# A hybrid attention and delta-rule layer on one core: the first weights fetched behind two input tiles, and the first two weight jobs' column blocks in another order

## Chip, core and metric

The kernel runs on one core of one Trainium2 chip. The metric is device time in microseconds of the whole launch; several runs are taken and their median is given. A profiled execution of the same kernel gives the rows quoted here; its times count from the start of its span.

## What is computed

The reference is one layer of a streaming encoder. A prompt of 2048 rows and a sample of 32 rows, each row 1024 wide, are normalised, projected by one wide matrix, sent through two branches (chunk-band attention and a gated delta rule) and merged:

```python
hp = layer_norm(x_prompt, ln0_g, ln0_b)          # 2048 x 1024
hs = layer_norm(x_sample, ln0_g, ln0_b)          #   32 x 1024
# in trunk_layer, for either of them:
qa, ka, va, za, qkv_b, zb, a_b, b_b, gate_a, gate_b = split_projection(x @ w_in)
...
mix = jax.nn.sigmoid(gate_a) * ya + jax.nn.sigmoid(gate_b) * yb
y = layer_norm(ALPHA * x + mix @ w_out, ln_g, ln_b)
```

Only the first step matters for this change: the normalisation of the first rows and the first products `x @ w_in`, which belong to the logits `gate_a` and `gate_b`.

## The kernel before

The projection is made weight tile by weight tile, the weights stationary in TensorE and the transposed rows moving: a **job** is one block of 128 columns of `w_in` (1024 x 128, 512 KB), multiplied with half of the rows. The prompt is split in two halves of 1024 rows; what follows is the first half. The rows come as eight input tiles x0 to x7 of 128 rows (512 KB each).

**Building h** (`build_h`, lines 465 to 560). For each input tile: a transfer into `x`; on VectorE two `bn_stats`, one `bn_aggr`, one small addition; on GpSimd the power -0.5; on VectorE the subtraction and scaling of the whole tile ("x<-x,mv" in the trace); on TensorE eight transposes, four into a bank of the tag `b` and four into one of the tag `a`; then ScalarE applies gain and bias to the first four (`tmp<-b`) and VectorE to the other four (`tmp<-a`); ScalarE casts `tmp` to f16 (`hi`), GpSimd forms the rest (`lo<-tmp,hi`). A column block of a job can start when `hi` of its tiles is there and ends with eight products that read `lo`.

**Fetching and dividing weights** (`fetch`, line 583; `divide`, line 613). `fetch` issues two transfers of 256 KB for each job into one of two `wraw` buffers. `divide` handles one job after the other: ScalarE squares the tile and sums it, a small product with `tiny` sums over partitions (`b<-w_sq,tiny`), then `w_scale` goes through VectorE, GpSimd (the power) and VectorE again, ScalarE scales `wraw` and casts it in two halves to `whi`, GpSimd forms `wlo`. There are two buffers of `whi` and `wlo`; a job's buffer comes free with the last product of its last column block.

**Multiplying** (`multiply`, line 657). A job's columns are cut in blocks, each 24 products: 16 with `hi` (with `whi` and `wlo`), then 8 with `lo`. The first job of a half is multiplied together with the second (`job.two`), block by block. The first two jobs of the first half are gate logits and have the blocks `FIRST[0]`: columns 0 to 255 (input tiles x0, x1), 256 to 511 (x2, x3) and 512 to 1023 (x4 to x7). Call the first job j0, the second j1, and the blocks b0, b1, b2. The third job is "ab" (64 columns instead of 128, blocks of 512 columns); the fourth is the first job of branch B. The product of a gate block goes through a tanh on ScalarE (`sig<-pj`) to DRAM.

**Who sets the order.** The kernel's Python runs a planner, `Flow`: each stream of work is a generator with a clock of its own, streams are resumed in the order of their clocks, every instruction is booked with an estimated price, and a transfer is booked at 200 GB/s plus a margin (line 206). The order in which the planner reaches the instructions is the order in which each engine executes them. Prices and due times therefore set the order, and the chip's waits set the times. `flow.start(gen, at)` starts a stream at a given clock.

**After the head.** The planner runs until the low part of tile x7 is issued (`flow.run(l_ready[0][7])`, line 2216). Then the Python function `phase_b(0)` opens the buffers of branch B, and issues 17 fillings with zeros on VectorE at that place:

```python
t = bp.tile([P, 8, P], F32, name=f"{name}{i}")
V.memset(t[:], 0.0)
...
k_bd, qk_bd = (diag(n, NPAR) for n in ("k_bd", "qk_bd"))     # NPAR = 4
q_bd, kd_bd, u_bd = (diag(n, NSIDE) for n in ("q_bd", "kd_bd", "u_bd"))   # NSIDE = 3
```

VectorE instructions that the planner reaches later stand behind them in VectorE's queue.

Of the kernel before, what the change touches and what calls it, by code (L numbers as in the profile page):

```python
# [56 lines left out]
for _p in range(1, NP):  # L57
# [9 lines left out]
FIRST = [  # L67
    [(0, 256, 0), (256, 256, 256), (512, 512, 512)],
    [(0, 256, 1024), (256, 256, 1280), (512, 272, 1536), (784, 272, 1808)],
]  # L70
# [197 lines left out]
def trunk(ctx: ExitStack, tc: tile.TileContext, x_p, x_s, cache_k, cache_v, st_conv, st_gdn,  # L268
# [4 lines left out]
    flow = Flow()  # L273
# [6 lines left out]
    def dma(dst, src, eng=nc.sync):  # L280

        eng.dma_start(dst, src)  # L282
        size = 2 if dst.dtype == F16 else 4
        n = size
        for k in dst.shape:
            n *= k

        n = max(n, n // (size * dst.shape[-1]) * 768)
        return flow.transfer("SP" if eng is nc.sync else "S", n)

    def gate(n):
        return Gate(flow, n)
# [4 lines left out]
    def mark():  # L297
        return Mark(flow)
# [166 lines left out]
    def build_h(half, xpool, nx):  # L465

        hT[half] = [None, None]
        ncols = HCOLS[half]
        nt = 4 - half
        x_gate, t_gate = gate(nx), gate(nt)  # L470
        freed, first = [mark(), mark()], mark()
        sizes = [SPLIT, ncols - SPLIT]
        tiles = [(n + P - 1) // P for n in sizes]

        def free(b):
            yield h_free[b]
            w = SPLIT if b == 0 else HALF + DEC - SPLIT
            hT[half][b] = [hpool.tile([P, KD, w], F16, tag=f"{x}{b}", name=f"{x}{half}{b}") for x in ("hi", "lo")]
            freed[b].done()

        def one(b, t, rows):
            c0 = t * P
            gt = half * 8 + b * 4 + t
            xt = xpool.tile([P, D], F32, tag="x", bufs=nx, name=f"x{gt}")
            yield dma(xt[:rows], x_s if rows < P else x_p[gt * P:(gt + 1) * P, :])
            if half == 0 and b == 1:
                yield first
            st = xpool.tile([P, 2, 6], F32, tag="st", bufs=nx, name=f"st{gt}")
            for i in range(2):
                V.bn_stats(out=st[:rows, i, :], in_=xt[:rows, i * 512:(i + 1) * 512])  # L490
                yield
            V.bn_aggr(out=mv[:rows, gt, :], in_=st[:rows])
            V.tensor_scalar(out=mv[:rows, gt, 1:2], in0=mv[:rows, gt, 1:2], scalar1=LN_EPS,
                            scalar2=None, op0=ALU.add)
            yield
            rsqrt(mv[:rows, gt, 1:2], mv[:rows, gt, 1:2])
            yield
            V.tensor_scalar(out=xt[:rows], in0=xt[:rows], scalar1=mv[:rows, gt, 0:1],
                            scalar2=mv[:rows, gt, 1:2], op0=ALU.subtract, op1=ALU.mult)
            yield freed[b]  # L500
            hi, lo = hT[half][b]
            todo = [2, 2, 2]

            def part(q):
                tag = "ba"[q] if half == 0 else "b"
                yield t_gate
                yield scaled
                yield bank[tag]
                tp = pt(tag)
                for k in range(4):  # L510
                    kk = 4 * q + k
                    PE.transpose(tp[:, k * P:k * P + rows], xt[:rows, kk * P:(kk + 1) * P],
                                 ident[:rows, :rows])
                todo[0] -= 1
                if not todo[0]:
                    x_gate.give()
                yield
                tmp = xpool.tile([P, 4, P], F32, tag="tmp", bufs=nt, name=f"tmp{gt}{q}")
                m = tmp[:, :, 0:rows]
                ks = slice(4 * q, 4 * q + 4)  # L520
                for k in range(4):
                    kk = 4 * q + k
                    src, g, b_ = tp[:, k * P:k * P + rows], ln0gT[:, kk:kk + 1], ln0bT[:, kk:kk + 1]
                    if q == 0:
                        S.activation(out=tmp[:, k, 0:rows], in_=src, func=AF.Identity, scale=g, bias=b_)
                    else:
                        V.tensor_scalar(out=tmp[:, k, 0:rows], in0=src, scalar1=g, scalar2=b_,
                                        op0=ALU.mult, op1=ALU.add)
                    if k == 1:
                        yield  # L530
                bank[tag].give()
                if b == 0 and t == 3 and q == 1:
                    first.done()
                yield
                hv_ = hi[:, ks, c0:c0 + rows]
                S.copy(out=hv_, in_=m)
                todo[1] -= 1
                if not todo[1]:
                    h_ready[half][gt - half * 8].done()
                yield  # L540
                (V if q == 0 and half == 1 else G).tensor_tensor(out=lo[:, ks, c0:c0 + rows], in0=m,
                                                                 in1=hv_, op=ALU.subtract)
                t_gate.give()
                yield
                todo[2] -= 1
                if not todo[2]:
                    l_ready[half][gt - half * 8].done()

            for q in range(2):
                flow.start(part(q))  # L550

        for b in range(2):
            flow.start(free(b))
        for b in range(2):
            if half == 0 and b == 1:

                yield 3.0
            for t in range(tiles[b]):
                yield x_gate
                flow.start(one(b, t, min(P, sizes[b] - t * P)))  # L560

# [95 lines left out]
    def multiply():  # L657

        while True:
            some, todo = [], [(0, 0)]  # L660
            while todo:
                bi, which = todo.pop(0)
                if which == len(some):
                    some.append((yield from q_w.get()))
                    job = some[which][0]
                    if which == 0:

                        todo = [(b, w) for b in range(len(job.blocks)) for w in range(1 + job.two)][1:]
                    if job.key:
                        job.open = mark()  # L670
                        flow.start(open_job(job))
                job, wh, wl = some[which]
                c0, n, gcol = job.blocks[bi]
                tiles = range(c0 // P, (c0 + n + P - 1) // P)
                for i in tiles:
                    yield h_ready[job.half][i]
                hh, hl = h_cols(job.half, c0, n)
                yield bank["pj"]
                ps = pt("pj")
                for k in range(KD):  # L680
                    PE.matmul(ps[:, 0:n], wh[:, k], hh[:, k, :], start=(k == 0), stop=False)
                    yield
                    if job.cols == P:
                        PE.matmul(ps[:, 0:n], wl[:, k], hh[:, k, :], start=False, stop=False)
                        yield
                for i in tiles:
                    yield l_ready[job.half][i]
                for k in range(KD):
                    PE.matmul(ps[:, 0:n], wh[:, k], hl[:, k, :], start=False, stop=(k == KD - 1))
                    if k == KD - 1:  # L690
                        last = bi == len(job.blocks) - 1
                        if job.end and (bi == 0 or last):
                            h_free[0 if bi == 0 else 1].give()
                        if last:
                            w_gate.give()
                    yield
                flow.start(evac(job, bi, c0, n, gcol, ps))
                if job.end and job.half == 1:
                    if last:
                        jobs_done.done()  # L700
                        flow.start(leave())
# [1503 lines left out]
    with ExitStack() as stack0:  # L2205
        open_banks(stack0, "ps0", a=3)
        xp = stack0.enter_context(tc.tile_pool(name="x0", bufs=1, reuse_waits="tile"))
        flow.start(norm_params(xp))
        flow.start(build_h(0, xp, 8))
        flow.start(fetch(marked()), 2.0)  # L2210
        flow.start(setup(xp), 20.0)
        flow.start(setup2(xp), 30.0)
        flow.start(spread(), 100.0)
        flow.start(divide())
        flow.start(multiply())
        flow.run(l_ready[0][7])
# [78 lines left out]
```

## Time and profile before

| | |
|---|---|
| Median of 3 runs | 2121.21 us (2118.57 to 2124.31) |
| Profiled execution, its own time | 2124.96 us |
| Its span | 2123.1 us |
| TensorE products busy | 1994.4 us (94% of the span) |
| VectorE busy | 1534.2 us (72%) |
| ScalarE busy | 978.7 us (46%) |
| GpSimd busy | 634.3 us (30%) |
| Transfers | 196.49 MB, mean 93 GB/s |

The engines are PE (TensorE, products and transposes), PEld (its weight loads), DVE (VectorE), ACT (ScalarE), POOL (GpSimd) and SP (which issues the transfers). In the rows of the timeline the columns are: start, duration, engine, source line, operation, output<-inputs, shapes, count, and in brackets the idle time of the engine before it with what ended it. Nearly all instructions are recorded by one helper, so their line is L259, and they are told apart by their tiles. In the table of stretches each engine has its busy time and the number of its instructions.

### The profile page before, as it was taken

The page shows a single profiled execution, that of the slowest core. Times are in us where ns is not written, and L with a number is a line of the kernel's source. Part 1 is how long each engine was busy: PE and PEld are TensorE (multiplying, and loading weights), DVE is VectorE, ACT ScalarE, POOL GpSimd, SP SyncE. Part 2 cuts the span into 40 slices and gives each one's busy share as a digit, 9 for nine tenths or more (in the row PEclk, how much of TensorE's full clock was granted, in tenths as well). Part 3 has the DMA queues.
Part 4 walks back from the last instruction along what each step waited for, and adds up shares of the span by engine and source line. Part 5 has one row for each costly group of instructions (what it writes and reads, how often), then busy time and mean ns, then how long its engine had stood idle before and what let it go on. Part 6 is the DMA issues. An engine that isn't in the chain of part 4 may idle for free. (4 is left out here: it accounts for less than half of the span.)

```text
span 2123.1 us, 41363 instructions
## 1 busy us (share of the span) xinstructions
PE 1994.4 (94%) x15098; PEld 1422.5 (67%) x15098; DVE 1534.2 (72%) x4660; ACT 978.7 (46%) x2098; POOL 634.3 (30%) x708
## 2 busy tenths in 40 slices
PE   4999898999999999999899999999999988999998
PEld 4454665666465656666666676767776777988896
DVE  7689989884277768779898987347657667766676
ACT  5655544443465667564444443346656652111110
POOL 6243333232322122333233232310110223443343
PEclk9999999899999999999999999999999999999999
DMA  3223232222423233222223233332322435443331
GB/s 120 75 84 102 76 88 78 67 79 82 122 67 120 82 93 99 70 73 76 58 70 94 62 86 85 99 100 72 92 77 67 138 120 191 128 123 103 116 107 61
DMA packets 197719, 196.49 MB, mean 93 GB/s; under 512 B 79622, under 2 KB 147570, under 8 KB 197516
## 3 DMA queue, kind: packets, MB, share of 16 engines
q1 hardware_dynamic: 197516, 193.85, 30.9%
q8 instruction: 119, 1.95, 0.4%
q14 instruction: 84, 0.69, 0.1%
HBM read 135.91 MB, written 50.53 MB: 88 GB/s over the span
## 5 line engine op out<-in xcount | busy, mean ns | idle before, releaser
L259 PE MATMUL pj<-hi,whi 128*128 128x512 f16 (+2 forms) x1992 | 650.7, 342 | 8.6 <-POOL whi L259 3.0
L259 PE MATMUL pj<-hi,wlo 128*128 128x512 f16 (+2 forms) x1952 | 640.8, 341 | 0.4 <-POOL wlo L259 0.4
L259 PEld LDWEIGHTS <-whi 128*128 128x128 f16 x3984 | 416.0, 106 | 217.5 <-issue 11.2
L259 PE MATMUL pj<-lo,whi 128*128 128x512 f16 (+2 forms) x1992 | 461.9, 340 | 0.0
L259 POOL TENSOR_TENSOR wlo<-wraw,whi 128x512 f16<-128x512 f32 x192 | 228.6, 1193 | 630.1 <-ACT whi L259 345.1
L259 PEld LDWEIGHTS <-wlo 128*128 128x128 f16 x1952 | 205.5, 105 | 108.5 <-issue 8.9
L259 ACT CAST mh<-sg 128x256 fp32r<-128x256 f32 x64 | 25.9, 407 | 276.1 <-DVE sg L259 276.0
L259 DVE TENSOR_TENSOR sys_u<-sys_u,sys_t 128x60 f32<-128x60 f32 (+24 forms) x527 | 135.7, 258 | 18.2
L259 PE MATMUL a<-ghi,whi 128*128 128x256 f32 (+1 forms) x512 | 134.8, 293 | 7.1 <-DVE sg L259 6.8
L259 ACT ACTIVATE wraw<-wraw,w_scale 128x1024 f32<-128x1024 f32 (+1 forms) x98 | 111.4, 1137 | 59.2 <-DVE w_scale L259 57.1
L259 ACT CAST ph<-b 128x512 f16<-128x512 f32 (+2 forms) x224 | 92.6, 422 | 92.7 <-PE b L259 86.1
L259 PE MATMUL a<-ghi,wlo 128*128 128x256 f32 (+1 forms) x512 | 131.9, 287 | 0.0
L259 ACT CAST whi<-wraw 128x512 f16<-128x512 f32 (+1 forms) x196 | 119.4, 611 | 27.1 <-PE pj L259 24.2
L259 DVE TENSOR_TENSOR pl<-b,ph 128x512 f16<-128x512 f32 (+2 forms) x224 | 107.6, 484 | 28.9 <-ACT ph L259 28.0
L259 DVE TENSOR_TENSOR sys_t<-sys_u,sys_p 128x54 f32<-128x54 f32 (+21 forms) x459 | 123.6, 269 | 4.0
L259 ACT ACTIVATE sb<-sb,mx,unit 128x640 f32<-128x640 f32 (+4 forms) x128 | 109.0, 852 | 25.5 <-DVE mx L259 25.1
L259 DVE SCALAR_TENSOR_TENSOR acc<-raw,cwT,acc 128x512 f32<-128x512 f32 x144 | 113.2, 786 | 8.4 <-ACT acc L259 7.4
L259 POOL TENSOR_TENSOR w_scale<-w_scale,mhalf 128x1 f32<-128x1 f32 x49 | 31.0, 633 | 288.0 <-DVE w_scale L259 230.1
L259 PEld LDWEIGHTS a<-ghi,whi 128*128 128x128 f32 x512 | 99.3, 194 | 8.8 <-DVE sg L259 7.9
L259 PE MATMUL b<-ident,sb 128*128 128x128 f32 x560 | 98.8, 276 | 2.9 <-ACT tmp L259 0.6
L259 ACT COPY v_t<-o 128x64 f32<-128x64 f32 x132 | 27.5, 209 | 158.3 <-PE o L259 121.5
L259 PEld LDWEIGHTS a<-ghi,wlo 128*128 128x128 f32 x512 | 98.9, 193 | 0.4 <-DVE wlo L259 0.2
(350 smaller groups left out, 4238.9 us busy)
## 6 DMA issues: line engine op xcount, KB each, us to landing
wraw<-in_w_in SPq DMA_DIRECT2D x192, 256.0 KB
sg<-sig SPq DMA_DIRECT2D x112, 128.0 KB
sig<-sig SPq DMA_DIRECT2D x44, 256.0 KB
sys_p<-sol_p SPq DMA_DIRECT2D x17, 512.0 KB
x<-in_x_p SPq DMA_DIRECT2D x16, 512.0 KB
xt<-in_x_p SPq DMA_DIRECT2D x16, 512.0 KB
out_y_p<-xt SPq DMA_DIRECT2D x16, 512.0 KB
glo<-g SPq DMA_DIRECT2D x14, 512.0 KB
```

The source lines that it names most:

```text
L259: r = f(*a, **k)
```

## The change

Three edits. In `build_h` the loop over the tiles of the first 512 rows waits until clock 2.0 before the third tile. The stream `fetch` starts at clock 1.0 instead of 2.0. Together the transfers are issued in the order x0, x1, the weights of j0, the weights of j1, x2, x3, x4 to x7; before, all of x0 to x3 stood ahead of the weights. In `multiply` the list of blocks of the first pair of jobs begins j0 b0, j0 b1, j1 b0, j1 b1 instead of j0 b0, j1 b0, j0 b1, j1 b1; j0 b2 and j1 b2 follow as before.

```diff
@@ build_h
             for t in range(tiles[b]):
+                if half == 0 and b == 0 and t == 2:
+                    yield 2.0
                 yield x_gate
                 flow.start(one(b, t, min(P, sizes[b] - t * P)))
@@ multiply
                         todo = [(b, w) for b in range(len(job.blocks)) for w in range(1 + job.two)][1:]
+                        if job.blocks is FIRST[0]:
+
+                            todo[:3] = [(1, 0), (0, 1), (1, 1)]
@@ start of the kernel
         flow.start(build_h(0, xp, 8))
-        flow.start(fetch(marked()), 2.0)
+        flow.start(fetch(marked()), 1.0)
         flow.start(setup(xp), 20.0)
```

## The prediction

> **What bounds the kernel now.** I read the page's busy shares first, then a table of stretches, then the timelines of the first 80 us engine by engine.
>
> ```profile
> PE 1994.4 (94%) x15098; PEld 1422.5 (67%) x15098; DVE 1534.2 (72%) x4660; ACT 978.7 (46%) x2098; POOL 634.3 (30%) x708
> ```
>
> ```profile
> 0.00:10.00 10.00, 1.97 (x9) 1.83 (x10) 6.10 (x24) 1.28 (x1) 1.97 (x9) 1.00 0.72 274
> 10.00:20.00 10.00, 4.94 (x22) 4.08 (x20) 7.66 (x20) 7.29 (x17) 5.77 (x7) 1.00 0.71 269
> 0.00:100.00 100.00, 68.28 (x402) 42.60 (x403) 70.07 (x175) 58.41 (x105) 44.71 (x56) 0.95 0.27 93
> ```
>
> TensorE is busy 94% of the span, so the kernel as a whole is paced by it; but in the first 100 us it is busy for 68.28 and stands for 31.7, and that is where the change works. On TensorE's own timeline the head looks like this:
>
> ```profile
> 32.09 0.42 PE L259 MATMUL pj<-hi,whi 128*128 128x256 f16 x1
> 32.30 0.42 PE L259 MATMUL pj<-hi,wlo 128*128 128x256 f16 x1
> ...
> 36.61 0.93 PE L259 MATMUL pj<-lo,whi 128*128 128x256 f16 x7
> ...
> 44.89 1.09 PE L259 MATMUL b<-ident,x 128*128 128x128 f32 x4 [5.97 <-ACT hi L259]
> ...
> 55.65 0.38 PE L259 MATMUL pj<-hi,whi 128*128 128x512 f16 x1
> ...
> 64.63 1.89 PE L259 MATMUL pj<-lo,whi 128*128 128x512 f16 x8
> 69.51 2.74 PE L259 MATMUL pj<-hi,whi 128*128 128x512 f16 x6 [2.99 <-POOL whi L259]
> ```
>
> j0 b0 runs from 32.09 to 37.5, its first products 0.21 us apart. Then TensorE stands for 5.97 us until the transposes of x7; the other three 256-column blocks follow, j0 b2 starts at 55.65, j1 b2 ends at 66.52, and the ab job waits 2.99 us for its weights. That last wait is the one to look at, since it is the only one of TensorE between 60 and 80 us:
>
> ```profile
> PE pj L259 <- POOL whi L259: 3.0, 1, 3.0
> ```
>
> The row blames GpSimd, but GpSimd only passes on a lateness. VectorE's timeline shows whose:
>
> ```profile
> 9.68 0.68 DVE L259 BATCH_NORM_STATS2 st<-x 128x6 f32<-128x512 f32 x1
> ...
> 13.76 0.68 DVE L259 BATCH_NORM_STATS2 st<-x 128x6 f32<-128x512 f32 x1
> ...
> 17.12 0.72 DVE L259 TENSOR_SCALAR tmp<-a,ln0gT,ln0bT 128x128 f32<-128x128 f32 x2
> ...
> 43.11 1.63 DVE L259 TENSOR_SCALAR x<-x,mv 128x1024 f32<-128x1024 f32 x1
> 46.94 1.36 DVE L259 TENSOR_SCALAR tmp<-a,ln0gT,ln0bT 128x128 f32<-128x128 f32 x4 [2.20 <-POOL wlo L259]
> 48.47 0.91 DVE L259 MEMSET k_bd<- 128x1024 f32 x1 [0.16 <-issue]
> ...
> 65.65 0.91 DVE L259 MEMSET u_bd<- 128x1024 f32 x1 [0.16 <-issue]
> 66.48 0.09 DVE L259 TENSOR_SCALAR w_scale<-b 128x1 f32<-128x1 f32 x1
> 67.25 0.15 DVE L259 TENSOR_SCALAR w_scale<-w_scale 128x1 int32<-128x1 int32 x1 [0.67 <-POOL w_scale L259]
> ```
>
> VectorE finishes the last part of x7 at 48.30, and then clears 17 buffers one behind the other, first at 48.47, last from 65.65 to 66.56: one every (65.65 - 48.47) / 16 = 1.074 us. The scale of the ab weights stands behind them. Its input had been on the way since ScalarE squared those weights:
>
> ```profile
> 47.61 1.34 ACT L259 CAST hi<-tmp 128x512 f16<-128x512 f32 x2
> ...
> 61.03 1.06 ACT L259 ACTIVATE whi<-wraw 128x1024 f16<-128x1024 f32 x1 [4.66 <-PE pj L259]
> ```
>
> The square was over at 62.1, the scale was taken at 66.48. So the ab job starts by this chain and no other: VectorE's last `tmp` of x7 (48.30), plus 18.2 us for the clearing (to 66.48), plus 3.0 us for the weights (to 69.51). The code makes the order unavoidable in the changed kernel as well: the clearing is issued when the low part of x7 is in the plan, the last block of j0 reads that low part, and only its last product frees the buffer into which the ab weights are divided.
>
> **The change part by part.**
>
> *What TensorE gains up to j1 b2.* x7's last `hi` cast ends at 48.95 (row above), and j0 b2 could start there instead of at 55.65 if the four small blocks were done: up to 6.7 us. They can be. The weights of j0 and j1 become whole when GpSimd ends their second `wlo`:
>
> ```profile
> 28.57 1.15 POOL L259 TENSOR_TENSOR wlo<-wraw,whi 128x512 f16<-128x512 f32 x1
> ...
> 45.72 1.15 POOL L259 TENSOR_TENSOR wlo<-wraw,whi 128x512 f16<-128x512 f32 x1
> ...
> 68.79 1.30 POOL L259 TENSOR_TENSOR whi<-wraw,whi 128x256 f16<-128x256 f32 x2 [1.57 <-ACT whi L259]
> ```
>
> that is at 29.72 and 46.87. The planner books 2.62 us for an input tile (524,288 bytes at 200 GB/s), so two tiles fewer ahead of the weights move j0's division 5.2 us forward in its order, clear of the work for x2 and x3. My estimate is j0's weights at 20 to 23 us and j1's at about 30, and then three cold blocks of 5.4 us (32.09 to 37.54) end at 46. I book this gain at 6.7 us, and it is worth nothing by itself: j1 b2 then ends at about 60, and TensorE waits for the ab weights, which hang on VectorE. Its wait of 2.99 grows to about 9.7. Everything turns on the moment at which VectorE ends x7.
>
> *What moves on VectorE.* Four terms.
>
> First, x2's two statistics (from 9.68) and the first of x3's (13.76) now run in gaps of x0 and x1. With x2 booked 5.2 us later, behind j0's weights, they fall behind x1's last `tmp`. That is three statistics of 0.68 and two small ones, 2.4 us of work that loses its cover. Against it x1 itself ends earlier: its `tmp` (17.12 to 17.84) has those statistics no longer ahead of it, which I put at 1.3 us, and the five small operations of j0's scale (0.8 us) move into the gap that is left. Net +0.3.
>
> Second, x2's transposes come to stand among j0 b0's products in TensorE's queue. Sixteen products at 0.21 us are 3.4 us; from j0's weights at about 20 they end at 23, while x2 would be ready for its transposes at about 21. VectorE's `tmp` of x2 waits for them: +1.7, between 0 (other statistics fill the gap) and 5.4 (a whole cold block ahead).
>
> Third, waits that go. VectorE's own rows between 15.6 and 48.4 us, by group, show what it loses in front of `tmp`:
>
> ```profile
> L259 DVE TENSOR_SCALAR tmp<-a,ln0gT,ln0bT 128x128 f32<-128x128 f32 x27 | 9.5, 401 | 5.8 <-PE a L259 2.2 <-POOL wlo L259 2.2 <-ACT whi L259 1.4
> ```
>
> 5.8 us in all. The last 2.2 of them are x7's own transposes and stay (the 44.89 row), nothing being behind them. The 1.4 at j0's `whi` should go, and of the 2.2 at the transposes about half: -2.5. If all but the last went, -3.6.
>
> Fourth, j1's scale: five small operations, 0.8 us, leave the stretch of x4 to x7 for the waits around x2 and x3, and count as -0.5 between 0 and -0.8.
>
> Sum: +0.3 + 1.7 - 2.5 - 0.5 = -1.0 us; with the small waits between groups that I cannot place (a few tenths each way) I take -0.5. Ends: everything good, 0.3 + 0 - 3.6 - 0.8 = -4.1; everything bad, 2.4 + 5.4 + 0 + 0 = +7.8.
>
> *What costs nothing.* x2 and x3 land later by the 1.05 MB of weights ahead of them: at 274 and 269 GB/s (rows above) 3.9 us. x2 was in use at 9.68, so it lands by 13.6 at the latest, and its turn on VectorE comes at about 16; if x1 ended before 13.6, that cover would be gone and the difference would be added. SP issues the same transfers in another order and holds no wait. ScalarE gets the tanh of the four blocks into its queue ahead of x5 to x7 instead of behind them, 0.47 each by the same form; if TensorE is late with a block, ScalarE stands there with x7's cast behind it, and that price lies within the +7.8.
>
> Two rules of the Trainium skill bear on the terms. TensorE's first products after the 2.99 us wait are slow already: six take 2.74 us (69.51 row). "TensorE: Matmul & The Clock Gate", section "HAM oscillation", gives as its rule no idle gaps above about 3.4 us. Read strictly, the gap of before should have stayed under it and one of 9.7 us goes over it, which would be a loss of half of 3.4, 1.7 us; by the row it is paid already and I add 0. The other is the shared port:
>
> ```profile
> L259 DVE TENSOR_SCALAR x<-x,mv x8: 798/856/1632, 7.9 to 43.1; 128x1024 f32<-128x1024 f32 x8
> ```
>
> The shortest of these takes 0.80 and the longest 1.63, the one at 43.11, during which GpSimd forms a `lo`. "SBUF — State Buffer", section "SBUF: two separate sides", says that whoever of VectorE and GpSimd starts first has the shared pair for the whole instruction. By it the 0.8 us would go if GpSimd, rid of j1's `wlo`, were idle then, and the sum would be -1.3; I leave the sum at -0.5, because GpSimd's `lo` of x5 and x6 falls there in either order.
>
> **How the sum stands to the runs.** The profiled execution took 2124.96 us (span 2123.1), 3.75 above the median of 2121.21. With -0.5 it would be 2124.5; against the median 2120.7. About 0.3%, 6.4 us, is what can be told from no change here.
>
> **Rivals.**
>
> *The idle is gained in full.* If the clearing did not bind, j0 b2 would start at 48.95 and everything behind it 6.7 us earlier, with the ab weights ready in time another 2.99: 2111.5 to 2114.5. For it speaks the wait on GpSimd that the waits name; against it VectorE's row at 66.48, which comes 0.08 us before the last clearing is over. Chance 0.05.
>
> *Transposes behind cold blocks.* If x2's and x3's transposes each come to stand behind a cold block (5.4 us each, of which VectorE can fill about 1.5 with x4's statistics), x7 ends 7 to 8 us later, the clearing starts later by as much, and the time is 2128 to 2129. It decides when more than 4 us of block products stand ahead of x2's transposes. For it speaks that the planner prices such a product at 0.107 us (256 / 2400) and the chip takes 0.21 here; against it that x2's share is six tiles before the end. Chance 0.13, two thirds of it above +6.4.
>
> *The order far behind the head changes.* The planner's clocks shift by a few microseconds against streams with fixed start times (the one that starts at 100.0), and a reordering of later work could move the time either way, 6 to 10 us: 2111 to 2131. Against it: by the ab job all engines have waited for one chain in the plan too, and from there on clocks shift together. Chance 0.18, half faster and nearly half slower.
>
> **Chances and range.** The head held by the clearing: 0.64, with its own range 2117 to 2124. Faster by over 0.3%: 0.05 + 0.09 + 0.02 from the good end of the likeliest, 0.16. Slower: 0.09 from the second rival, 0.08 from the third, 0.17. Within 0.3%: 0.67. The range 2113 to 2129 takes in both ends of the VectorE sum and the nearer parts of the rivals.
>
> **What would show it.** On TensorE j0 b0 starts between 20 and 24, all four small blocks are done before x7's transposes, j0 b2 starts within 2 us of 49, and the wait before the ab job is 8 to 11 us instead of 2.99. On VectorE the 17 clearings start within 3 us of 48.5 and the ab scale follows the last one at once. From the ab job on the timeline is that of before, shifted by less than 3 us. The prediction is wrong if the ab scale no longer follows the clearing directly, if the clearing starts before 44 or after 55, or if the shift at the ab job is not the shift at the end.

## The result and the profile after

The changed kernel takes 2133.51 us (median of 6 runs, 2129.5 to 2139.21), the kernel before 2120.32 us (median of 6 runs beside it, 2117.85 to 2124.31). The ratio is 1.0063, with a 95% interval of 1.0049 to 1.0077: slower by 13.2 us, outside the predicted range of 2113 to 2129.

One caution before the rows: the profiled execution of the changed kernel was its quickest (2129.5 us), and that of the kernel before its slowest here (2124.96 us). Between the two traces lie only 4.4 us of span, so places can be compared in them, totals cannot.

The head of the program went much as predicted. TensorE's timeline of the changed kernel:

```profile
19.74 0.40 PE L259 MATMUL pj<-hi,whi 128*128 128x256 f16 x1 [4.18 <-ACT whi L259]
...
44.69 0.93 PE L259 MATMUL pj<-lo,whi 128*128 128x256 f16 x7
...
51.59 0.57 PE L259 MATMUL pj<-hi,whi 128*128 128x512 f16 x1 [4.12 <-ACT hi L259]
...
62.26 1.89 PE L259 MATMUL pj<-lo,whi 128*128 128x512 f16 x8
70.92 2.74 PE L259 MATMUL pj<-hi,whi 128*128 128x512 f16 x6 [6.77 <-POOL whi L259]
```

j0 b0 starts at 19.74 instead of 32.09, the four small blocks are through before x7's transposes, j0 b2 starts at 51.59 instead of 55.65, j1 b2 ends at 64.15 instead of 66.52. Then TensorE waits 6.77 us instead of 2.99, and the ab job starts at 70.92, 1.41 us later than before. VectorE's timeline shows the same holder as before:

```profile
48.35 1.37 DVE L259 TENSOR_SCALAR tmp<-a,ln0gT,ln0bT 128x128 f32<-128x128 f32 x4 [0.27 <-POOL lo L259]
49.88 0.91 DVE L259 MEMSET k_bd<- 128x1024 f32 x1 [0.16 <-issue]
...
67.06 0.91 DVE L259 MEMSET u_bd<- 128x1024 f32 x1 [0.16 <-issue]
67.89 0.10 DVE L259 TENSOR_SCALAR w_scale<-b 128x1 f32<-128x1 f32 x1
```

x7's last `tmp` ends at 49.72 (before 48.30), plus 18.2 us of clearing to the scale at 67.89, plus 3.0 us to the products at 70.92: the sum that the prediction wrote, with its first term 1.42 us larger. Executions of one and the same head differ too: the first clearing starts at 48.47, 47.77 and 47.61 in three traces with the head of before, at 49.88, 49.47 and 49.70 in three with the changed head, so the shift of the head lies between 1 and 2.3 us.

The loss lies far behind. This table of stretches is of the kernel before, then of the changed one (columns: stretch, length, then busy time and count of PE, PEld, DVE, ACT and POOL, clock granted to TensorE as a share of full speed, share of the DMA engines, GB/s):

```profile
540.00:600.00 60.00, 60.00 (x309) 28.56 (x307) 20.32 (x80) 29.96 (x55) 19.85 (x21) 1.00 0.34 103
700.00:830.00 130.00, 128.15 (x1050) 79.27 (x1049) 86.48 (x330) 87.05 (x186) 21.77 (x23) 0.99 0.27 80
830.00:880.00 50.00, 46.77 (x398) 35.65 (x397) 43.89 (x90) 32.21 (x71) 20.93 (x24) 1.00 0.33 105
```

```profile
540.00:600.00 60.00, 55.17 (x263) 25.65 (x261) 19.78 (x75) 24.99 (x45) 19.01 (x20) 0.94 0.33 96
700.00:830.00 130.00, 129.63 (x1090) 79.91 (x1088) 89.84 (x347) 86.76 (x189) 21.18 (x23) 1.00 0.28 81
830.00:880.00 50.00, 44.38 (x341) 32.38 (x340) 41.63 (x85) 32.03 (x70) 24.05 (x25) 0.97 0.32 98
```

Where TensorE had no idle time at all before, between 540 and 600 us, it now stands for 4.83 us and its clock falls to 0.94. Between 830 and 880 us, where the second half's rows are normalised, it loses another 2.39 us, but between 700 and 830 us it stands 1.48 us less than before, so most of that is paid back. The large place is the first. No part of the change touches work at these times.

### The profile page after: what moved, and what is told of

The parts are those of the page before. It is cut to its first block, busy times and chain, and to the rows that moved or that the text cites. A ratio compares the mean times of both kernels' runs of the same rounds, so it can differ in the third digit from the quotient of the medians.

```text
span 2127.5 us, 41393 instructions
## 1 busy us (share of the span) xinstructions
PE 1996.4 (94%) x15098; PEld 1417.1 (67%) x15098; DVE 1529.6 (72%) x4660; ACT 978.2 (46%) x2098; POOL 632.3 (30%) x708
## 5 line engine op out<-in xcount | busy, mean ns | idle before, releaser
L259 DVE TENSOR_TENSOR sys_t<-sys_u,sys_p 128x54 f32<-128x54 f32 (+20 forms) x459 | 117.9, 257 | 4.1
L259 DVE CUSTOM_DVE_ANT_0 sb<-a,bias 128x320 f32<-128x320 f32 (+4 forms) x128 | 61.4, 486 | 50.9 <-PE a L259 50.1
```

The costliest lines, as they stand in the source:

```text
L259: r = f(*a, **k)
```

## The experiments

Each run stands beside runs of the kernel before on the same chip: medians of 2120.42 us (25 runs) for the first four told here, 2120.3 us (35 runs) for the version with the bias rows at 92.0 and the three with a shared clearing, 2120.93 us (28 runs) for the one with another gate job and the three with clearing streams. The question behind the first four: is the loss in the head, or in the written order behind it? The planner's clocks at the end of the head are 4.991 later in the changed kernel than before; that is a number of its own Python code, not of the chip. One stream behind the head, `spread`, which sends the bias rows to DRAM 20 clock units apart, starts at a clock written in the code (100.0) and not relative to the head. Against it, all the rest is now planned 4.991 later. For short, the "written order" is the order of the instructions on each engine, and the "head" is all that comes before the ab job.

**Only the order of the blocks.** The two edits of the fetch order are left out.

```diff
+                        if job.blocks is FIRST[0]:
+                            todo[:3] = [(1, 0), (0, 1), (1, 1)]
```

> Only the order of the first pair's blocks is changed; transfers and fetch as before. Outside some 20 instructions in the head the written order on every engine is that of the kernel before. Theory (the ab job starts when VectorE has ended x7 and cleared 17 buffers, and what the whole change lost behind the head comes from a changed written order there): ab job within 0.5 us of 69.5, whole time within 3 us of the kernel before (2117 to 2124). Rival (the new block order itself costs, by cold products or late tanh): 2125 or more.

Measured: 2119.7 us (12 runs), ratio 0.9998 [0.9985, 1.0011]. TensorE's timeline of this kernel, j1's last block and the ab job:

```profile
61.78 1.89 PE L259 MATMUL pj<-lo,whi 128*128 128x512 f16 x8
68.74 2.74 PE L259 MATMUL pj<-hi,whi 128*128 128x512 f16 x6 [5.06 <-POOL whi L259]
```

j1 b2 ends 2.85 us earlier than before (64.63 to 61.78 for the row of its last products), and the wait takes 2.07 of that away. The ab job is 0.77 us earlier, which misses the expected 0.5 by a little; the first clearing starts at 47.70 here, within 0.1 us of where it starts in two other traces of the head of before, so this is no gain of the swap. TensorE's gain is worth nothing while the clearing holds the ab scale; this step of the prediction stands. The swap by itself is not the loss.

**Only the two edits of the fetch order.**

```diff
             for t in range(tiles[b]):
+                if half == 0 and b == 0 and t == 2:
+                    yield 2.0
...
-        flow.start(fetch(marked()), 2.0)
+        flow.start(fetch(marked()), 1.0)
```

> Only the two edits of the fetch (third input tile at clock 2.0, weights at clock 1.0); blocks in the old order. From the ab job on the written order is the same as in the changed kernel. Theory: as slow as the changed kernel, 2130 to 2137, with the ab job 1 to 2 us later than before. Rival (the block order costs): between, 2120 to 2127.

Measured: 2133.46 us (6 runs), ratio 1.0064 [1.004, 1.0087], as slow as the whole change, with the ab job at 70.55. These two edits carry the loss, by the head or by the order.

**The whole change, with the order behind the head put back.** The start of `spread` is moved along with the head, so that all streams behind the head stand to each other as before.

```diff
-        flow.start(spread(), 100.0)
+        flow.start(spread(), 104.991037)
```

> The changed kernel, with the one stream of the planner that starts at a fixed clock behind the head (the bias rows, clock 100.0) started 4.991 later, which is the shift of the planner's clocks by the change. So the head is that of the changed kernel and the written order behind it is that of the kernel before. Theory (written order behind the head): the head's 1.4 us alone stays, 2120 to 2125. Rival (the head's own cost, cold products or a later branch B, carries through): 2130 to 2137.

Measured: 2122.69 us (12 runs), ratio 1.0013 [1.0002, 1.0024]. With the order of before, the change costs 2.3 us. The traces show that the order is that of before: from the ab job on, VectorE, ScalarE, GpSimd and the queue of transfers on SP have the same list of instructions, one by one, in this run and in the kernel before.

**The kernel before, with the changed kernel's order.** No part of the change, only the start of `spread`.

```diff
-        flow.start(spread(), 100.0)
+        flow.start(spread(), 95.008963)
```

> The kernel before, with that stream started 4.991 earlier (95.009). So the head is that of the kernel before and the written order behind it is that of the changed kernel. Theory: slow without any of the change, 2128 to 2135, with the ab job at 69.5. Rival: as the kernel before, 2117 to 2124.

Measured: 2131.17 us (8 runs), ratio 1.0045 [1.0028, 1.0062]: 10.7 us slower with an untouched head. From the ab job on these lists are those of the changed kernel, one by one; against the kernel before they differ on the three engines between 138 and 861 us, and in the queue of transfers from 90 us on. The ab job starts at 68.81, with the head of before. The four corners close: 2.3 for the head and 10.7 for the order make 13.0, and the whole change measured 13.2. That they close so well is luck, for the intervals reach from 0.4 to 5.1 and from 5.9 to 13.1 us. The stretches 540 to 600 and 830 to 880 us in the changed kernel with the old order, then in the kernel before with the new order:

```profile
540.00:600.00 60.00, 60.00 (x297) 28.04 (x294) 18.84 (x75) 29.67 (x52) 19.42 (x21) 1.00 0.36 106
830.00:880.00 50.00, 46.78 (x392) 34.98 (x390) 44.01 (x92) 33.35 (x73) 21.03 (x24) 1.00 0.37 109
```

```profile
540.00:600.00 60.00, 55.17 (x263) 25.74 (x262) 19.56 (x74) 25.06 (x44) 18.53 (x20) 0.94 0.33 96
830.00:880.00 50.00, 44.40 (x341) 32.37 (x339) 41.36 (x86) 32.51 (x71) 24.05 (x25) 0.97 0.32 96
```

To 0.02 us the idle time of TensorE in these two stretches follows the order and not the head. What ends it is in TensorE's waits of the changed kernel, in the first stretch and in the second (columns: what was waited for, us in total, times, longest):

```profile
PE pj L259 <- ACT vf L259: 3.5, 1, 3.5
PE b L259 <- ACT whi L259: 1.3, 1, 1.3
```

```profile
PE b L259 <- DVE tmp L259: 3.0, 2, 1.8
PE pj L259 <- POOL wlo L259: 1.0, 2, 0.6
```

The first stretch is the seam between branch B and attention in the first half. The changed kernel's ScalarE and TensorE there:

```profile
554.54 1.06 ACT L259 ACTIVATE whi<-wraw 128x1024 f16<-128x1024 f32 x1 [6.19 <-issue]
...
557.23 1.15 ACT L259 ACTIVATE wraw<-wraw,w_scale 128x1024 f32<-128x1024 f32 x1 [1.54 <-DVE w_scale L259]
558.41 0.62 ACT L259 CAST whi<-wraw 128x512 f16<-128x512 f32 x1
558.93 1.26 ACT L259 ACTIVATE vf<-pj,w_inv 128x512 f32<-128x512 f32 x2
...
559.66 0.58 PE L259 MATMUL pj<-hi,whi 128*128 128x512 f16 x1 [3.54 <-ACT vf L259]
...
563.77 0.38 PE L259 MATMUL pj<-hi,whi 128*128 128x512 f16 x1
```

ScalarE has been idle for 6.19 us before 554.54, yet the two banks of the first attention job are emptied (`vf<-pj`) only at 558.93, because in ScalarE's queue the next job's weights stand ahead: square, scale and cast. ScalarE's timeline has no emptying of a bank between 545.07 and 558.93, and in that time TensorE ends two blocks, the last at 554.45. Both banks of `pj` are full until then, and TensorE stands. Afterwards it is slow as well: the ten products from 559.66 on take 4.11 us, 0.41 each, where 0.22 each is usual (the block of j0 b2 in the kernel before). So the seam costs 4.83 us of standing and about 2.0 of slow products, 6.8 us by this estimate. In the kernel before, one of the two emptyings is already done at 550.83 and stands between the casts:

```profile
550.83 0.69 ACT L259 ACTIVATE vf<-pj,w_inv 128x512 f32<-128x512 f32 x1 [0.97 <-PE pj L259]
551.42 0.61 ACT L259 CAST whi<-wraw 128x512 f16<-128x512 f32 x1
```

SP's timeline shows how far branch B had come, by its last issue of `g<-gb` in this half, in the kernel before and in the changed one:

```profile
537.38 1.29 SPq L282 DMA_DIRECT2D g<-gb  x2
```

```profile
550.64 1.28 SPq L282 DMA_DIRECT2D g<-gb  x2
```

In the new order branch B is 13 us later at this point. (Two other traces have 551.07 with the new order and 531.50 with that of before.) The code ties the two together: `open_job` (line 644) lets an attention job's emptying into the plan only after `enter(0, half, make)`, which stands behind `flow.run(done)` of branch B. While the plan has not reached the end of branch B, the weights of further jobs go into ScalarE's queue ahead of the emptying, and the job that TensorE goes on to finds its banks full.

**One more gate job ahead of the seam.** If the place is right, another job between branch B and attention should cover it. The changed kernel takes seven gate jobs there instead of six.

```diff
-HEAD, TAIL = [2, 3], [6, 6]
+HEAD, TAIL = [2, 3], [7, 6]
```

> The changed kernel with one gate job more (7 instead of 6) ahead of the first attention job of the first half. It tests the seam between branch B and the attention, where TensorE waits 1.3 and 3.5 us in the changed kernel because branch B ends late against the jobs. Theory (the jobs ran ahead of branch B): with one more job between, the two waits go and the time falls by 4 to 7 us, 2126 to 2130. Rival (the wait is the first attention job's own): the waits stay and the time is 2131 to 2137.

Measured: 2126.52 us (12 runs), ratio 1.0029 [1.0014, 1.0044], 7.0 us less than the 2133.5 of the changed kernel, which stood beside other runs of the kernel before; its interval, 1.0049 to 1.0077, does not reach this one. Up to 547 us the order on the three engines is that of the changed kernel. Its stretches:

```profile
540.00:600.00 60.00, 60.00 (x293) 28.50 (x293) 17.66 (x62) 25.85 (x41) 20.68 (x21) 1.00 0.38 114
700.00:830.00 130.00, 128.42 (x1063) 80.33 (x1061) 92.58 (x351) 88.39 (x191) 24.79 (x26) 1.00 0.30 87
830.00:880.00 50.00, 43.81 (x403) 34.20 (x402) 41.39 (x100) 30.95 (x72) 18.55 (x21) 0.97 0.29 88
```

The seam is busy without a gap again, as the theory said, and the second stretch is not better. The 7.0 us agree with the 6.8 read from the rows, but they are not a clean price: the extra job moves later work as well (between 700 and 830 us TensorE stands 1.58 us, where the changed kernel stands 0.37), and the kernel before was not run with the extra job. The rest of the 10.7 us was not tried by itself and no one place in the traces accounts for it.

**Another start of the bias rows.** Is an earlier start always bad? The kernel before with a start at 92.0.

```diff
-        flow.start(spread(), 100.0)
+        flow.start(spread(), 92.0)
```

> The kernel before with nothing changed but the start of the bias rows' stream, 92.0 instead of 100.0. The head is that of the kernel before; the written order behind it is a third one. Theory (the written order behind the head moves the time by several microseconds in either direction): a time that differs from the kernel before by more than 3 us, the planner's own end time being 4.5 earlier: 2110 to 2118. Rival (only the one order that the change made was bad, others are alike): 2118 to 2123.

Measured: 2122.56 us (12 runs), ratio 1.0013 [0.9999, 1.0026]. It isn't: 100.0 gives 2120.3, 95.0 gives 2131.2, 92.0 gives 2122.6, and the last cannot be told from the first. These three starts show no slope, only one order that is worse than two others; the theory's larger effect was missed.

**Sharing the clearing with GpSimd.** If the clearing holds the ab job, seven of the 17 fillings on GpSimd should free it, in the kernel before and more in the changed one. In all versions from here on the start of `spread` is set for the order meant: that of before, or that of start 92.0.

```diff
-                V.memset(t[:], 0.0)
+                (G if half == 0 and (name, i) in CLEAR_G else V).memset(t[:], 0.0)
```

> The kernel before, with 7 of the first half's 17 clearings on GpSimd and 10 on VectorE; the bias rows' stream starts at 97.995, which keeps the written order behind the head that of the kernel before. Theory (the clearing alone holds the ab job): the scale of ab no longer follows a clearing but its own sum, the weights are there at about 65.6, and the ab job follows j1 b2 without a wait at 66.5 instead of 69.5, warm: 2121.2 less 3.0 and less about 1.6 for the cold products, 2115 to 2118. Rival (GpSimd or the weights' chain itself is late): a wait of 2 to 3 us stays and the time is 2119 to 2123.

> The whole change, the same sharing of the clearing, and the bias rows' stream at 102.986, so that the written order behind the head is that of the kernel before. Theory: j1 b2 ends at about 64.1 as in the changed kernel and the ab job follows at once: 5.4 earlier than before and warm, 2112 to 2116, and 2 to 3 us under the run with the same clearing and the old head. Rival (the change's head costs something that the clearing hid): as the other or above, 2116 to 2122.

Measured: in the kernel before 2122.11 us (12 runs), ratio 1.0009 [0.9996, 1.0023], nothing gained; in the changed kernel 2115.87 us (12 runs), ratio 0.9982 [0.997, 0.9994]. The first is a miss, and its rows say why (VectorE, ScalarE, TensorE):

```profile
63.38 0.16 DVE L260 TENSOR_SCALAR w_scale<-b 128x1 f32<-128x1 f32 x1 [4.07 <-PE b L260]
...
67.33 0.69 ACT L260 ACTIVATE sig<-pj,w_half 128x512 f32<-128x512 f32 x1 [3.86 <-issue]
67.92 0.71 ACT L260 ACTIVATE wraw<-wraw,w_scale 128x512 f32<-128x512 f32 x1
...
69.87 1.96 PE L260 MATMUL pj<-hi,whi 128*128 128x512 f16 x6 [2.62 <-POOL whi L260]
```

The scale is there at 63.38, 3.1 us earlier than before, and VectorE even waits 4.07 us for it. But on ScalarE the scaling of the ab weights stands behind j1 b2's tanh (`sig<-pj`), which needs the end of j1 b2. The clearing had hidden a second holder, at nearly the same time, as the kernel before has it too:

```profile
66.61 0.69 ACT L259 ACTIVATE sig<-pj,w_half 128x512 f32<-128x512 f32 x1 [3.85 <-issue]
```

That tanh ends at 67.30, the last clearing at 66.56. As long as ScalarE's queue has this order, the ab job starts about 2.6 us after j1 b2 ends, whatever VectorE does. In the changed kernel j1 b2 ends earlier, and there the shared clearing pays:

```profile
65.56 1.47 PE L260 MATMUL pj<-hi,whi 128*128 128x512 f16 x6 [2.57 <-POOL whi L260]
```

With the shared clearing the changed head is 6.2 us quicker than the head of before (2115.87 against 2122.11, and the two intervals do not overlap), where 2 to 3 us were expected. The ab job's start, 65.56 instead of 69.87, shows 4.3 of them.

**The same with the third order.** The changed kernel, shared clearing, and the order of start 92.0 (here 94.985662).

> The whole change, the shared clearing, and the written order of the run with the stream at 92.0 behind the head (94.986 here, for the planner's clocks are 2.986 later). Theory: head and order add up, so this run differs from the one with the change and the shared clearing by as much as the run at 92.0 differs from the kernel before: 2106 to 2114. Rival (they do not add): within 2 us of the run with the change and the shared clearing.

Measured: 2115.45 us (12 runs), ratio 0.9968 [0.9953, 0.9982]; below the other order by 0.4 us, which is nothing. The expectation of 2106 to 2114 was missed, and the rival's "within 2 us" holds.

**Both holders taken away.** The fillings become two streams of the planner, ten on VectorE and seven on GpSimd, that give way after each one. Then the ab scale comes in between, and the scaling of the ab weights is reached ahead of j1 b2's tanh.

```diff
+        def clearing(eng, tiles):
+            for t in tiles:
+                eng.memset(t[:], 0.0)
+                yield
...
+        for eng, tiles in zip((V, G), clear):
+            flow.start(clearing(eng, tiles))
```

> The kernel before with the two clearing streams, bias rows' stream at 88.848, the written order behind the head that of the kernel before. Theory (the scaling of ab behind j1 b2's tanh kept the gain of the shared clearing at zero): now the ab job follows j1 b2 within 1 us, at 66.5 to 67.5 instead of 69.5: 2116 to 2119, 2 to 4 above the same with the change. Rival: 2119 to 2123 as before.

> The whole change; the 10 clearings on VectorE and the 7 on GpSimd are two streams of the planner, so the scales of the next jobs come in between, and on ScalarE the scaling of the ab weights stands ahead of j1 b2's tanh. The bias rows' stream starts at 90.075, which keeps the written order behind the head that of the kernel before. Theory (with the shared clearing alone, ScalarE's queue held the ab weights behind j1 b2's tanh for 2.6 us): the ab job follows j1 b2 within 1 us, at 63 to 64, 5.5 to 6.5 earlier than before: 2112 to 2116. Rival (the head no longer counts, branch B waits for something else): 2116 to 2121.

> As the run with the two clearing streams and the change, with the written order of the run at 92.0 behind the head (82.075 here). Theory: 1 to 3 us under the run with the change, the shared clearing and that order (2115.5): 2111 to 2115. Rival: the same as that run or above it, 2115 to 2119.

Measured, with the order of before: 2116.83 us (12 runs), ratio 0.9979 [0.9967, 0.9991], without the change; 2114.73 us (10 runs), ratio 0.9969 [0.9955, 0.9983], with it. With the change and the order of start 92.0: 2113.12 us (7 runs), ratio 0.9959 [0.9943, 0.9975], which has the lowest median of all and is quicker than the kernel before by its interval. All three lie in the ranges of their theories. ScalarE and TensorE in the version with the change and the order of before:

```profile
62.38 0.72 ACT L260 ACTIVATE wraw<-wraw,w_scale 128x512 f32<-128x512 f32 x1 [2.32 <-DVE w_scale L260]
...
63.86 0.69 ACT L260 ACTIVATE sig<-pj,w_half 128x512 f32<-128x512 f32 x1 [0.32 <-PE pj L260]
...
61.93 1.89 PE L260 MATMUL pj<-lo,whi 128*128 128x512 f16 x8
64.34 1.04 PE L260 MATMUL pj<-hi,whi 128*128 128x512 f16 x4 [0.52 <-POOL whi L260]
```

The scaling of the ab weights now stands ahead of the tanh, and the wait of 6.77 us has become 0.52, with 0.26 behind the first four products. Without the change the ab job starts at 65.22 with no wait, earlier than expected, and then waits 0.96 us. With the clearing and the tanh out of the way, the change is worth 2116.83 - 2114.73 = 2.1 us in the medians (the two intervals overlap), where with the clearing in place it cost 2.3. The two orders behind the head, 2114.73 and 2113.12, cannot be told apart.

## Why the prediction was wrong

**Right: what holds the ab job.** The clearing stood between x7 and the ab scale as forecast (18.2 and 3.0 us, both to a tenth). The forecasts for TensorE's rows: j0 b0 at 20 to 24 (19.74), j0 b2 within 2 of 49 (51.59, missed by 0.6), the wait 8 to 11 us (6.77, missed because j1 b2 ended at 64.15 and not at 60), a shift of less than 3 us at the ab job (1.41). j0 b2 started late because ScalarE's last `hi` casts of x7 end at 52.06 instead of 48.95. The prediction had named one sign of being wrong that came true: the shift at the ab job (1.41) is not the shift at the end (13.2).

**Mis-sized: the sum on VectorE.** Forecast -0.5, measured +1.42 in the traces, and +2.3 (0.4 to 5.1 by the interval of 1.0002 to 1.0024) for the whole head by the run with the old order. Two terms failed. VectorE's groups between 16 and 49.8 us, in the kernel before (one row), then in the changed one:

```profile
L259 DVE TENSOR_SCALAR x<-x,mv 128x1024 f32<-128x1024 f32 x6 | 6.7, 1118 | 0.0
```

```profile
L259 DVE TENSOR_SCALAR tmp<-a,ln0gT,ln0bT 128x128 f32<-128x128 f32 x27 | 9.5, 402 | 4.4 <-PE a L259 3.2 <-ACT tmp L259 0.9 <-POOL lo L259 0.3
L259 DVE TENSOR_SCALAR x<-x,mv 128x1024 f32<-128x1024 f32 x6 | 5.5, 911 | 2.8 <-POOL mv L259 2.6
```

The waits saved nothing in sum. From 16 us to the end of x7 VectorE stands 7.6 us in the kernel before and 7.7 in the changed one, while the second to fourth terms together forecast -1.3. In front of `tmp` the waits fell from 5.8 to 4.4 us, and those at the scales and some small operations by 1.2. But a wait that the list of terms did not have appeared: 2.8 us in front of `x<-x,mv`, 2.6 of it for GpSimd's power, which now stands behind the forming of `wlo` and `lo` on that engine.

The first term, put at +0.3, was the larger miss. It counted three statistics without cover. VectorE's timeline of the kernel before has two more operations ahead of x1's last `tmp` (the row at 17.12 in the prediction), a fourth statistic and the scaling of x2:

```profile
15.61 0.68 DVE L259 BATCH_NORM_STATS2 st<-x 128x6 f32<-128x512 f32 x1
16.21 0.99 DVE L259 TENSOR_SCALAR x<-x,mv 128x1024 f32<-128x1024 f32 x1
```

In the changed kernel all of these come behind x1's last `tmp`, which ends at 16.82, the first three statistics together:

```profile
18.22 1.88 DVE L259 BATCH_NORM_STATS2 st<-x 128x6 f32<-128x512 f32 x3
```

That is about 3.5 us of work instead of 2.4. x1 ended 1.0 us earlier (16.82 instead of 17.84) and not 1.3, and j0's scale found no gap. By this estimate the term comes to about +2.5.

Against that the six `x<-x,mv` became 1.2 us shorter in this pair of traces (0.4 against another trace of the head of before, where the six take 5.9). The prediction named the shared port as a thing worth 0.8 us and left it out. "SBUF — State Buffer", section "SBUF: two separate sides", of the Trainium skill says that where VectorE, in some kinds of instruction, and GpSimd meet on the shared pair, the first to start holds it for its whole instruction. The direction agrees with it: the two longest of the kernel before, 1.58 us at 36.12 and 1.63 at 43.11, run while GpSimd forms a `lo`. No run tests it by itself.

**Did not happen: transposes behind cold blocks.** x7 ended 1.4 us later, not 7 to 8. **Excluded rightly: the idle gained in full.**

**The step that failed: "the order far behind the head changes".** It was a rival with a chance of 0.18, priced at 6 to 10 us, and split evenly between both signs. Against it the prediction said that "from there on clocks shift together". They do, by 4.991, for all streams but the one that the rival itself named, which starts at a fixed 100.0. That sentence took the shift to be harmless because it was uniform; but a uniform shift against a fixed start is a change of order, and whether it comes is not a matter of chance: two numbers in the code decide it. Which sign it has they do not tell. It measured +10.7 us (1.0028 to 1.0062), a little over the rival's size. So the likeliest case was right about the head and wrong about all that follows it, where the prediction booked nothing. From the ab job on the timeline was therefore not "that of before, shifted by less than 3 us".

**Open.** The traces show where the new order loses and what TensorE waits for there, and the code shows why the emptying stands behind branch B. Why the position of eight small transfers lets branch B fall behind by 13 us isn't settled. Nor was the second stretch, 830 to 880 us, tried alone.

## What to carry to other kernels

Where a planner writes the order, an edit has two prices, one at its place and one in the order of all that is planned after it; look for starts and due times that do not move with the edit, and test the two prices apart, the old head with the new order and the new head with the old one. An instruction that is late because one queue holds it may be held by a second queue right behind: here the clearing on VectorE and a tanh on ScalarE ended within a microsecond, and taking away the first alone gained nothing. A gain that ends in a wait is not lost for good: the same change cost 2.3 us with both holders in place, gained 6.2 with the clearing shared, and about 2 with both gone.

## What was not expected of the hardware

TensorE's products were slow after a wait of less than 3 us. Six ab products took 1.47 us after a wait of 2.57, 1.96 after 2.62, 2.74 after 2.99 (rows above and in the prediction). After 2.85, in the kernel before with the new order, TensorE's row is:

```profile
68.81 2.52 PE L259 MATMUL pj<-hi,whi 128*128 128x512 f16 x6 [2.85 <-POOL whi L259]
```

"TensorE: Matmul & The Clock Gate", section "HAM oscillation", of the Trainium skill gives about 3.4 us as the gap to stay under; here products were slow after gaps of 2.62 to 2.99 us. The length of the wait does not decide alone. After the 2.57 us the granted clock stays at 1.00 for the next 6 us, but in another place of the kernel before, among other short waits, 2.11 us were enough (TensorE's row, then the stretch that follows):

```profile
894.51 1.13 PE L259 MATMUL b<-ident,ab 40*64 40x40 f32 x32 [2.11 <-DVE ab L259]
```

```profile
895.50:898.90 3.40, 3.40 (x18) 1.73 (x15) 1.30 (x6) 1.40 (x3) 1.15 (x5) 0.50 0.49 139
```

The same written order had another clock from one execution to the next. Between 355 and 425 us, in the kernel before and in the one with only the blocks reordered, whose orders differ in the head alone:

```profile
355.00:425.00 70.00, 62.90 (x427) 43.56 (x425) 60.34 (x216) 30.58 (x66) 18.82 (x25) 0.90 0.25 67
```

```profile
355.00:425.00 70.00, 63.24 (x459) 43.64 (x459) 63.84 (x238) 33.36 (x71) 19.45 (x26) 0.98 0.26 70
```

0.90 and 0.98 of the clock over 70 us is a difference of about 5.6 us, which is in line with runs of one kernel that lie up to 8 us to either side of their median (35 runs of the kernel before: 2115.38 to 2128.18, median 2120.3). A difference of 0.3% cannot be read from two traces; it took the medians of 6 to 12 runs beside 25 to 35 of the kernel before.
